# The entry of a two-layer hybrid decoder: another way to sum the squares of x, multiplications of zeros at the start, and the second chunk of a projection ahead of the decay's small matmuls

## The chip, the core and the metric

One core of one Trainium2 chip. The metric is the device time of one execution in microseconds (us); the lower, the better. The kernel before has three timed runs, and one more execution that was profiled.

## What is computed

The input x has 256 tokens of 2048 channels. Two layers follow each other, each a mixer and a squared-ReLU MLP, with an RMSNorm before and after each. Only the first steps of layer 0 matter here:

```
y    = x * rsqrt(mean(x^2 over channels) + eps) * w       # rmsnorm
proj = y @ w_in                                           # 2048 x 8208
q,k,v,z | beta,a | ... = split(proj)                      # gated DeltaNet and retention
g    = -exp(a_log) * softplus(a + dt_bias)                # decay, 8 heads
G    = cumsum(g) in chunks;  decay = exp(G_t - G_s)       # used by the delta rule
```

The factor rsqrt(...) is one number per token, so it can be put on after the product `x*w @ w_in`, when the result is taken out of PSUM. The kernel does that: the product starts on x itself, and the factor (`rstd`, one column per block of 128 tokens) is needed only when the first results leave PSUM.

## The kernel before

All matmuls of the projections are float32 split in two: ScalarE rounds a weight tile `raw` to `whi` (line 125), VectorE subtracts to get the rest `wlo` (line 126), and TensorE makes three products of each tile, `xh*whi`, `xl*whi` and `xh*wlo` (lines 132, 133, 134). x is split in the same way into `xh` (ScalarE, line 192) and `xl` (VectorE, line 193).

A chunk of the projection is some 384 to 512 columns wide. It runs over 16 tiles of 128 channels, in four weight groups of four tiles, and over two blocks of 128 tokens: 96 matmuls. A weight group is one DMA from HBM on SyncE's queue, or several for the first groups (`PARTS`: four for the first, two for the second, one for each of the others). There are three `raw` buffers, so a group's DMA waits until VectorE has made the `wlo` of the group three before it.

The entry of layer 0 (`layer0_mixer`) loads x transposed (`xT`, eight DMAs of two channel tiles each into tiles `xs` with the tag kq), splits it, and makes the first chunk, 400 columns: 16 for beta and the decay and 384 of the gate z. GpSimd squares each `xs` tile (lines 512 and 515) and adds the squares to `sq` (line 516, tag Bn). When the last is added, four matmuls with a column of ones (line 527) sum `sq` over channels, and `rstd` follows (lines 530 and 185). The first chunk then leaves PSUM, and a chain of small steps on VectorE and ScalarE makes the decay `g`. One small matmul (line 569) sums it up, and 16 more (line 585, in four banks) spread it for the 256 exponentials' tiles.

The second chunk of the entry (384 more columns of z) stands behind these small matmuls in the program's text. A list scheduler of the framework fixes the order of each engine's queue when the kernel is built: of what it takes to be ready it puts the earliest in the text first. In the trace the second chunk's matmuls start before the decay is ready, and the small matmuls stand among them. Then come the chunks for k, q and v of the delta rule.

Of the kernel before, what the change touches and what calls it, by code (L numbers as in the profile page):

```python
# [12 lines left out]
AF = mybir.ActivationFunctionType  # L13
ALU = mybir.AluOpType
# [3 lines left out]
P = 128  # L18
D = 2048
SEQ = 256  # L20
HID = 4 * D
SGW = 2 * D
EPS = 1e-6
# [6 lines left out]
PARTS = [4, 2, 1, 1]  # L30
WAIT = [26, 30]
AHEAD = 200
SEVEN, KEPT = (0, 2), 1
ORDER = (None, 0, None, 1, None, 2, None, 3)
FIRST = (None, None, 1, None, 0, None, 3, 2)
# [58 lines left out]
def program(tc, nc, A, S):  # L94
    wp = tc.alloc_tile_pool(name="wp", bufs=1)
    cp = tc.alloc_tile_pool(name="cp", bufs=1)
# [5 lines left out]
    mxp = tc.alloc_tile_pool(name="mxp", bufs=2, space=PSUM)  # L102
    V, G, ACT, PE, DMA = nc.vector, nc.gpsimd, nc.scalar, nc.tensor, nc.sync
# [3 lines left out]
    def T(pool, shape, tag, dt=F32, bufs=None):  # L107
        uid[0] += 1
        kw = {} if bufs is None else {"bufs": bufs}
        return pool.tile(shape, dt, tag=tag, name=f"{tag}_{uid[0]}", **kw)  # L110

    def bank(pool, n, tag):
        return T(pool, [P, 512], tag)[:, :n]

    def weights(s, blocks, parts=1):
        src, width = s.take(blocks)
        raw = T(wp, [P, 2048], "raw", bufs=RAW_BUFS)[:, :width]
        hi = T(wp, [P, 2048], "whi", F32R, bufs=HI_BUFS)[:, :width]
        lo = T(wp, [P, 2048], "wlo", F32R, bufs=LO_BUFS)[:, :width]
        with tc.high_priority(offset=ahead[0]):  # L120
            n = width // parts
            for c in range(0, width, n):
                r, a, d = raw[:, c : c + n], hi[:, c : c + n], lo[:, c : c + n]
                DMA.dma_start(r, src[:, c : c + n])
                ACT.activation(a, r, AF.Copy)  # L125
                V.tensor_tensor(d, r, a.bitcast(F32), ALU.subtract)  # L126
        return hi, lo

    def prod_tok(ps, x, b, w, j, n, first, last):
        xh, xl = x[0][:, b * P : (b + 1) * P], x[1][:, b * P : (b + 1) * P]  # L130
        wh, wl = w[0][:, j * n : (j + 1) * n], w[1][:, j * n : (j + 1) * n]
        PE.matmul(ps, xh, wh, start=first, stop=False)  # L132
        PE.matmul(ps, xl, wh, start=False, stop=False)  # L133
        PE.matmul(ps, xh, wl, start=False, stop=last)  # L134
# [7 lines left out]
    def tick():  # L142
        clock[0] += 1
        while queue and queue[0][0] <= clock[0]:
            gen = heapq.heappop(queue)[2]
            delay = next(gen, None)
            if delay is not None:
                spawn(delay, gen)
# [6 lines left out]
    def chunk_tok(s, X, rows, spans, n, ps=None, first=True, last=True):  # L155
        if ps is None:
            ps = [bank(acc, n, "acc") for _ in range(2)]
        for u in range(0, len(rows), 4):
            w = weights(s, [(r, spans) for r in rows[u : u + 4]])
            for j in range(4):  # L160
                k = u + j
                for b in range(2):
                    prod_tok(ps[b], X[k], b, w, j, n, first and k == 0, last and k == len(rows) - 1)
                tick()
        return ps
# [10 lines left out]
    one = T(cp, [P, 1], "one")  # L176
# [3 lines left out]
    def small(n, tag, bufs=4):  # L180
        return T(cp, [P, n], tag, bufs=bufs)

    def rsqrt(out, x):
        n = x.shape[1]
        G.tensor_tensor(out, x, m05[:, :n], ALU.pow)

    def split(hi, lo, src, col=None):
        if col is None:
            ACT.activation(hi, src, AF.Copy)  # L189
            V.tensor_tensor(lo, src, hi.bitcast(F32), ALU.subtract)  # L190
        else:
            ACT.activation(hi, src, AF.Copy, scale=col)
            V.scalar_tensor_tensor(lo, src, col, hi.bitcast(F32), ALU.mult, ALU.subtract)
# [4 lines left out]
    def kts(groups):  # L198
        return [(e[0][:, j, :], e[1][:, j, :]) for e in groups for j in range(4)]
# [105 lines left out]
    ALLK = [k * P for k in range(NKT)]  # L305
# [181 lines left out]
    def layer0_mixer():  # L487
        rstd = [T(cp, [P, 1], f"rh{b}", bufs=2) for b in range(2)]
        s = S["la_in"]
        with tc.tile_pool(name="l0", bufs=1, reuse_waits="tile") as lp:  # L490
            xg = new_x()
            X = kts(xg)
            spans0 = [(4096, 16), (3072, 384)]
            ps = [bank(acc, 400, "acc") for _ in range(2)]
            xs = [T(lp, [P, 2, SEQ], "kq", bufs=8) for _ in range(8)]
            sq = T(lp, [P, 2, SEQ], "Bn", bufs=1)

            def load_x(i):
                DMA.dma_start(xs[i], A["xT"][:, i * 512 : (i + 1) * 512].rearrange("p (a t) -> p a t", a=2))
# [3 lines left out]
            for g in range(4):  # L503
                w = weights(s, [(r, spans0) for r in ALLK[g * 4 : g * 4 + 4]], parts=PARTS[g])
                for i in range(2 * g, 2 * g + 2):
                    if i < 7:
                        load_x(i + 1)
                    for a in range(2):
                        k = 2 * i + a
                        split(X[k][0], X[k][1], xs[i][:, a, :], nwc[:, k : k + 1])  # L510
                    if i == 0:
                        G.tensor_tensor(sq, xs[i], xs[i], ALU.mult)
                    else:
                        t = T(lp, [P, 2, SEQ], "PT", bufs=2)
                        G.tensor_tensor(t, xs[i], xs[i], ALU.mult)
                        G.tensor_tensor(sq, sq, t, ALU.add)
                if g == 3:
                    DMA.dma_start(ident, A["cst"][:, C_IDENT : C_IDENT + P])
                    lc = T(lp, [P, C_END - P], "lc")
                    DMA.dma_start(lc, A["cst"][:, P:C_END])  # L520
                for j in range(4):
                    for b in range(2):
                        prod_tok(ps[b], X[g * 4 + j], b, w, j, 400, g + j == 0, g * 4 + j == NKT - 1)
            pss = bank(mxp, 2, "mx")
            for b in range(2):
                for a in range(2):
                    PE.matmul(pss[:, b : b + 1], sq[:, a, b * P : (b + 1) * P], one, start=a == 0, stop=a == 1)
            for b in range(2):
                var = small(1, "var")
                V.tensor_scalar(var, pss[:, b : b + 1], 1.0 / D, EPS, ALU.mult, ALU.add)  # L530
                rsqrt(rstd[b], var)
            tri = lc[:, C_TRI - P : C_TRI]
            neg = lc[:, C_NEG - P : C_NEG]
            mk = [lc[:, C_M1 - P : C_M1], lc[:, C_M2 - P : C_M2]]
# [3 lines left out]
            zt = [[None] * 4 for _ in range(2)]  # L538
# [41 lines left out]
            for b in range(2):  # L580
                for hg in range(2):
                    ps4 = bank(mxp, 512, "mx")
                    for q in range(4):
                        c = (hg * 4 + q) * 2 + b
                        PE.matmul(ps4[:, q * P : (q + 1) * P], g2[:, c : c + 1].to_broadcast([P, P]), tri,
                                  start=True, stop=True)
# [11 lines left out]
                    for q in range(4):  # L598
                        c = (hg * 4 + q) * 2 + b
                        ACT.activation(e4[:, q, :], e4[:, q, :], AF.Exp, bias=ngc[:, c : c + 1])  # L600
            last_exp = ACT.activation(etail, etail, AF.Exp)

            ps = chunk_tok(s, X, ALLK, [(3072 + 384, 384)], 384)
            for b in range(2):
                ACT.activation(zt[b][0][:, 384:512], ps[b][:, 0:128], AF.Copy, scale=rstd[b])
                ACT.activation(zt[b][1][:, 0:256], ps[b][:, 128:384], AF.Copy, scale=rstd[b])
            with tc.issue_after(last_exp.ins):
                for b in range(2):
                    ACT.activation(zt[b][0], zt[b][0], AF.Silu)
# [255 lines left out]
            RQ, RK, RV, RG = 4112, 5136, 6160, 7184  # L865
            ahead[0] = AHEAD
            GT = [
# [20 lines left out]
            ps = chunk_tok(s, X, ALLK, [(3072 + 768, 256)], 256)  # L888
# [102 lines left out]
            for c in range(4):  # L991
                ps = chunk_tok(so, Og, ALLK[:12], [(c * 512, 512)], 512)
# [14 lines left out]
    def layer1_mixer(X, rh):  # L1007
        si, so = S["sg_in"], S["sg_out"]
        with tc.tile_pool(name="sg", bufs=1, reuse_waits="tile") as gp:
# [75 lines left out]
            return down_last(so, gts[7], rows(7), w1, w0, lambda b: rows_in(["e0", "e1"]), None)  # L1085

    X, rh, rv = layer0_mixer()
    X, rh, rv = ffn(S["up0"], S["dn0"], X, rv, 1, 5)
    X, rh, rv = layer1_mixer(X, rh)
# [58 lines left out]
```

## Time and profile before

| what | us |
|---|---|
| median of three runs | 2547.78 (2545.24 to 2547.9) |
| the profiled execution | 2548.88 |
| its span, first to last instruction | 2547.1 |
| TensorE busy in it | 2506.0 (98%) |
| VectorE, ScalarE, GpSimd busy | 1968.8, 1201.2, 285.8 |

The span is what the rows below are taken from. The profiled execution lasted 1.8 us longer than its span. Matmuls are pipelined, and their ends are modelled; so the distance from one start to the next tells more of TensorE's pace than the duration does.

### The profile page before, as it was taken

How to read it: one execution, taken by the hardware profiler on the slowest of the kernel's cores; microseconds unless marked ns; L12 is line 12 of the kernel's file. 1: busy time of each engine (PE TensorE's matmuls, PEld its weight loads, DVE VectorE, ACT ScalarE, POOL GpSimd, SP SyncE). 2: the span in 40 equal slices, each digit the busy share in tenths (PEclk: the TensorE clock that was granted, in tenths of full speed). 3: DMA queues.
4: the chain of work that ended last, by engine and by line, in shares of the span. 5: the costliest groups of instructions: out<-in, count | busy, mean ns of one | idle time of the engine just before them, and what ended most of it. 6: DMA issues, size and time to landing. Idle time of an engine off the chain costs nothing.

```text
span 2547.1 us, 36465 instructions
## 1 busy us (share of the span) xinstructions
PE 2506.0 (98%) x15138; PEld 2211.3 (87%) x15138; DVE 1968.8 (77%) x2256; ACT 1201.2 (47%) x1174; POOL 285.8 (11%) x222
## 2 busy tenths in 40 slices
PE   8999999999999999999999999999999999999998
PEld 7778888878999999999878877777789999999997
DVE  7586855579888888888854596876898888888887
ACT  6555444454454454545544333333544544445453
POOL 3000201140000000000310110110400000000001
PEclk9999999999999999999999999999999999999999
DMA  6444544544555455555555455555445554555553
GB/s 245 181 151 147 187 162 175 204 155 174 195 195 199 183 204 192 190 192 205 204 204 194 170 203 202 190 202 199 149 165 199 189 206 185 198 192 189 191 201 139
DMA packets 81255, 478.04 MB, mean 188 GB/s; under 512 B 13633, under 2 KB 15809, under 8 KB 26817
## 3 DMA queue, kind: packets, MB, share of 16 engines
q1 hardware_dynamic: 81088, 475.70, 51.1%
q8 instruction: 119, 1.95, 0.3%
q14 instruction: 48, 0.39, 0.0%
HBM read 473.04 MB, written 2.62 MB: 187 GB/s over the span
## 4 chain that ended last, share of the span: by engine, by line
PE 45%; DVE 4%; POOL 1%; issue 1%; ACT 0%; DVEq 0%; POOLq 0%; ACTq 0%
PE acc L133 9%; PE acc L134 9%; PE acc L132 9%; PE tp L318 4%; PE tp L319 4%; PE tp L320 4%; PE acc L362 1%; PE acc L364 1%; PE acc L363 1%; DVE wlo L126 1%; PE mx L363 1%; PE mx L362 1%; PE mx L364 1%; DVE h L275 1%; DVE bc L218 1%
## 5 line engine op out<-in xcount | busy, mean ns | idle before, releaser
L126 DVE TENSOR_TENSOR wlo<-raw,whi 128x2048 fp32r<-128x2048 f32 (+3 forms) x380 | 860.3, 2267 | 269.1 <-ACT whi L125 267.1
L125 ACT ACTIVATE whi<-raw 128x2048 fp32r<-128x2048 f32 (+3 forms) x380 | 714.1, 1880 | 566.3 <-PE acc L133 319.2
L318 PE MATMUL tp<-xh,whi 128*128 128x256 f32 x1920 | 539.5, 281 | 0.0
L319 PE MATMUL tp<-xl,whi 128*128 128x256 f32 x1920 | 539.2, 281 | 0.0
L320 PE MATMUL tp<-xh,wlo 128*128 128x256 f32 x1920 | 538.9, 281 | 0.0
L132 PE MATMUL acc<-whi,xh 128*128 128x512 f32 (+3 forms) x1120 | 446.3, 398 | 5.8 <-ACT whi L125 5.8
L134 PE MATMUL acc<-wlo,xh 128*128 128x512 f32 (+3 forms) x1120 | 440.0, 393 | 5.1 <-DVE wlo L126 5.1
L133 PE MATMUL acc<-whi,xl 128*128 128x512 f32 (+3 forms) x1120 | 438.9, 392 | 0.0
L318 PEld LDWEIGHTS tp<-xh,whi 128*128 128x128 f32 x1920 | 361.5, 188 | 2.7
L319 PEld LDWEIGHTS tp<-xl,whi 128*128 128x128 f32 x1920 | 361.6, 188 | 2.5
L320 PEld LDWEIGHTS tp<-xh,wlo 128*128 128x128 f32 x1920 | 361.7, 188 | 0.0
L134 PEld LDWEIGHTS acc<-wlo,xh 128*128 128x128 f32 x1120 | 212.1, 189 | 53.2 <-DVE wlo L126 7.0
L132 PEld LDWEIGHTS acc<-whi,xh 128*128 128x128 f32 x1120 | 212.4, 190 | 51.8 <-ACT whi L125 6.3
L133 PEld LDWEIGHTS acc<-whi,xl 128*128 128x128 f32 x1120 | 212.3, 190 | 44.7 <-issue 1.0
L387 POOL TENSOR_TENSOR rl<-rl 128x512 f32<-128x512 f32 x64 | 83.0, 1313 | 1261.0 <-ACT rl L386 1136.3
L189 ACT ACTIVATE whi<-qsum 128x2048 fp32r<-128x2048 f32 x60 | 115.3, 1922 | 179.9 <-DVE qsum L343 178.9
L190 DVE TENSOR_TENSOR wlo<-qsum,whi 128x2048 fp32r<-128x2048 f32 x60 | 138.7, 2312 | 79.0 <-ACT whi L189 77.0
L416 DVE TENSOR_TENSOR y<-acc,y 128x512 f32<-128x512 f32 x112 | 76.9, 687 | 86.1 <-PE acc L364 86.1
L189 ACT ACTIVATE whi<-raw 128x1536 fp32r<-128x1536 f32 x60 | 89.6, 1493 | 108.2 <-DMA raw<-dn 79.0
L133 PE MATMUL acc<-whi,e1l 128*128 128x512 f32 x288 | 114.0, 396 | 0.0
L134 PE MATMUL acc<-wlo,e1h 128*128 128x512 f32 x288 | 113.8, 395 | 0.0
L132 PE MATMUL acc<-whi,e1h 128*128 128x512 f32 x288 | 113.7, 395 | 0.0
(350 smaller groups left out, 4212.8 us busy)
## 6 DMA issues: line engine op xcount, KB each, us to landing
raw<-up SPq DMA_DIRECT2D x128, 1024.0 KB, 4.8
raw<-dn SPq DMA_DIRECT2D x128, 1024.0 KB, 4.8
raw<-sg_in SPq DMA_DIRECT2D x64, 1024.0 KB, 4.8
raw<-la_in SPq DMA_DIRECT2D x56, 1024.0 KB, 4.8
raw<-sg_out SPq DMA_DIRECT2D x32, 1024.0 KB, 4.8
raw<-la_out SPq DMA_DIRECT2D x16, 1024.0 KB, 4.8
raw<-la_in SPq DMA_DIRECT2D x4, 768.0 KB, 4.4
kq<-xT SPq DMA_DIRECT2D x8, 256.0 KB, 6.1
```

What stands on the lines that cost most here:

```text
L125: ACT.activation(a, r, AF.Copy)
L126: V.tensor_tensor(d, r, a.bitcast(F32), ALU.subtract)
L132: PE.matmul(ps, xh, wh, start=first, stop=False)
L133: PE.matmul(ps, xl, wh, start=False, stop=False)
L134: PE.matmul(ps, xh, wl, start=False, stop=last)
L189: ACT.activation(hi, src, AF.Copy)
L190: V.tensor_tensor(lo, src, hi.bitcast(F32), ALU.subtract)
L318: PE.matmul(out, wh[:, col], xh, start=k == 0 and m % 2 == 0, stop=False, skip_group_check=True)
L319: PE.matmul(out, wh[:, col], xl, start=False, stop=False, skip_group_check=True)
L320: PE.matmul(out, wl[:, col], xh, start=False, stop=k == NKT - 1, skip_group_check=True)
L387: G.tensor_tensor(r, r, r, ALU.mult)
L416: V.tensor_tensor(Y[key], ps, Y[key], ALU.add)
```

## The change

Four things. GpSimd no longer squares x. Behind the first chunk's loop x is loaded a second time, token-major, in four DMAs of 128 tokens by 1024 channels, and ScalarE squares each with a sum over its row (`accum_out`). The tiles have the tag PT, of which there are two buffers. `rstd` is made from the two sums of each token block, so that the four matmuls of line 527 are gone. Ten matmuls of a 128x128 tile of zeros are put at the very start (`WARM`), into a PSUM bank that nothing reads. The second chunk is moved in the text from behind the decay to ahead of it; its results are taken out where they were before.

```diff
+WARM = 10
...
             xs = [T(lp, [P, 2, SEQ], "kq", bufs=8) for _ in range(8)]
-            sq = T(lp, [P, 2, SEQ], "Bn", bufs=1)
+            heat = T(cp, [P, P], "heat")
+            G.memset(heat, 0.0)
+            cold = bank(mxp, P, "mx")
+            for _ in range(WARM):
+                PE.matmul(cold, heat, heat, start=True, stop=True)
...
                         split(X[k][0], X[k][1], xs[i][:, a, :], nwc[:, k : k + 1])
-                    if i == 0:
-                        G.tensor_tensor(sq, xs[i], xs[i], ALU.mult)
-                    else:
-                        t = T(lp, [P, 2, SEQ], "PT", bufs=2)
-                        G.tensor_tensor(t, xs[i], xs[i], ALU.mult)
-                        G.tensor_tensor(sq, sq, t, ALU.add)
...
-            pss = bank(mxp, 2, "mx")
             for b in range(2):
-                for a in range(2):
-                    PE.matmul(pss[:, b : b + 1], sq[:, a, b * P : (b + 1) * P], one, start=a == 0, stop=a == 1)
-            for b in range(2):
-                var = small(1, "var")
-                V.tensor_scalar(var, pss[:, b : b + 1], 1.0 / D, EPS, ALU.mult, ALU.add)
+                ssx = small(2, "ssx")
+                for c in range(2):
+                    xt = T(lp, [P, 1024], "PT", bufs=2)
+                    DMA.dma_start(xt, A["x"][b * P : (b + 1) * P, c * 1024 : (c + 1) * 1024])
+                    ACT.activation(xt, xt, AF.Square, accum_out=ssx[:, c : c + 1])
+                base, var = small(1, "base"), small(1, "var")
+                V.tensor_scalar(base, ssx[:, 0:1], 1.0 / D, EPS, ALU.mult, ALU.add)
+                V.tensor_scalar(var, ssx[:, 1:2], 1.0 / D, base, ALU.mult, ALU.add)
                 rsqrt(rstd[b], var)
+            psz = chunk_tok(s, X, ALLK, [(3072 + 384, 384)], 384)
...
             last_exp = ACT.activation(etail, etail, AF.Exp)
 
-            ps = chunk_tok(s, X, ALLK, [(3072 + 384, 384)], 384)
             for b in range(2):
-                ACT.activation(zt[b][0][:, 384:512], ps[b][:, 0:128], AF.Copy, scale=rstd[b])
-                ACT.activation(zt[b][1][:, 0:256], ps[b][:, 128:384], AF.Copy, scale=rstd[b])
+                ACT.activation(zt[b][0][:, 384:512], psz[b][:, 0:128], AF.Copy, scale=rstd[b])
+                ACT.activation(zt[b][1][:, 0:256], psz[b][:, 128:384], AF.Copy, scale=rstd[b])
```

## Rows read from the trace of the kernel before

**Rows 1.** The page's first part: busy time, share of the span, instructions.
```profile
PE 2506.0 (98%) x15138; PEld 2211.3 (87%) x15138; DVE 1968.8 (77%) x2256; ACT 1201.2 (47%) x1174; POOL 285.8 (11%) x222
```

**Rows 2.** Engine busy time by stretch: PE, PEld, DVE, ACT, POOL; TensorE's clock; DMA share, GB/s.
```profile
10.00:15.00 5.00, 3.66 (x13) 3.33 (x12) 5.00 (x5) 3.45 (x6) 4.84 (x4) 1.00 0.99 388
25.00:30.00 5.00, 3.67 (x12) 3.64 (x13) 5.00 (x6) 1.48 (x1) 3.51 (x2) 0.66 0.44 157
40.00:45.00 5.00, 5.00 (x35) 4.73 (x34) 4.26 (x12) 4.95 (x6) 0.00 (x0) 1.00 0.66 249
```

**Rows 3.** Who waited for whom in the first 38 us: total, times, longest.
```profile
ACT whi L125 <- DMA raw<-la_in: 9.4, 5, 3.6
PE acc L134 <- DVE wlo L126: 5.1, 4, 2.6
```

**Rows 4.** VectorE in order of time: start, duration of all merged, instruction.
```profile
4.51 0.98 DVE L193 SCALAR_TENSOR_TENSOR xl<-kq,par,xh 128x256 fp32r<-128x256 f32 x2 [3.55 <-ACT xh L192]
5.42 0.56 DVE L126 TENSOR_TENSOR wlo<-raw,whi 128x400 fp32r<-128x400 f32 x1
10.26 2.92 DVE L193 SCALAR_TENSOR_TENSOR xl<-kq,par,xh 128x256 fp32r<-128x256 f32 x2
13.10 3.40 DVE L126 TENSOR_TENSOR wlo<-raw,whi 128x400 fp32r<-128x400 f32 x2
29.59 1.81 DVE L126 TENSOR_TENSOR wlo<-raw,whi 128x1600 fp32r<-128x1600 f32 x1
31.32 0.87 DVE L193 SCALAR_TENSOR_TENSOR xl<-kq,par,xh 128x256 fp32r<-128x256 f32 x2
```

**Rows 5.** GpSimd's groups in the first 38 us: count, busy us and mean ns.
```profile
L516 POOL TENSOR_TENSOR Bn<-Bn,PT 128x512 f32<-128x512 f32 x7 | 10.4, 1484 | 0.5
L515 POOL TENSOR_TENSOR PT<-kq 128x512 f32<-128x512 f32 x7 | 10.4, 1482 | 2.8 <-DMA kq<-xT 2.8
```

**Rows 6.** TensorE in order of time, the matmuls alone.
```profile
5.36 0.70 PE L132 MATMUL acc<-whi,xh 128*128 128x400 f32 x1 [5.36 <-ACT whi L125]
14.85 0.34 PE L132 MATMUL acc<-whi,xh 128*128 128x400 f32 x1
...
15.04 0.35 PE L133 MATMUL acc<-whi,xl 128*128 128x400 f32 x1
...
17.06 0.54 PE L132 MATMUL acc<-whi,xh 128*128 128x400 f32 x1
...
17.39 0.54 PE L133 MATMUL acc<-whi,xl 128*128 128x400 f32 x1
...
36.01 0.95 PE L527 MATMUL mx<-one,Bn 128*128 128x1 f32 x8
36.82 0.42 PE L132 MATMUL acc<-whi,xh 128*128 128x384 f32 x1
...
43.19 0.40 PE L569 MATMUL mx<-g,lc 128*128 128x16 f32 x2
43.44 2.03 PE L585 MATMUL mx<-lc,g 128*128 128x128 f32 x16
```

**Rows 7.** SyncE's queue in order of time: start, time to issue, DMA.
```profile
7.93 1.19 SPq L499 DMA_DIRECT2D kq<-xT  x2
14.54 0.33 SPq L124 DMA_DIRECT2D raw<-la_in  x1
```

**Rows 8.** ScalarE in order of time.
```profile
9.41 0.53 ACT L125 ACTIVATE whi<-raw 128x400 fp32r<-128x400 f32 x1
15.12 1.54 ACT L125 ACTIVATE whi<-raw 128x1600 fp32r<-128x1600 f32 x1 [0.97 <-DMA raw<-la_in]
20.09 1.54 ACT L125 ACTIVATE whi<-raw 128x1600 fp32r<-128x1600 f32 x1 [1.83 <-DMA raw<-la_in]
```

**Rows 9.** ScalarE's groups of the whole span: a pass over 1024 columns, and the accumulator's reading.
```profile
L189 ACT ACTIVATE f0h<-tr 128x1024 fp32r<-128x1024 f32 x16 | 16.8, 1047 | 6.8 <-DVE tr L401 6.8
L227 ACT ACTIVATION_READ_ACCUMULATOR junk<-y 128x1 f32 x32 | 6.0, 188 | 0.0
```

## Prediction

> **What bounds the kernel now.** The page's busy shares come first: TensorE has 2506.0 of 2547.1 us [rows 1]. All that is not TensorE's is 41 us, so an edit can win only where TensorE waits or runs at a low clock. The table by stretches shows one such place in the entry. From 10 to 15 us and from 25 to 30 us TensorE is busy 3.66 and 3.67 of 5 us, and the clock granted falls to 0.66 in the second; from 40 us on it is busy all the time at 1.00 [rows 2]. In both early stretches VectorE is busy 5.00 of 5 us, and GpSimd 4.84 and 3.51 [rows 2]. The waits of the entry say the same: TensorE waits for VectorE's `wlo` [rows 3].
>
> VectorE's order of time shows why it is full. Two `xl` of 128x256 take 0.98 us at 4.51 and 0.87 us at 31.32, but 2.92 us at 10.26: 1.46 us each in place of some 0.46. A `wlo` of 400 columns takes 0.56 us at 5.42; at 13.10 one of 400 and one of 800 columns (the row names the first) take 3.40 us [rows 4], where 0.56 + 1.0 would be expected from the widths. Between 10 and 28 us GpSimd runs its squares and sums, 15 operations of 1.0 to 1.5 us [rows 5]. When they are over, 1600 columns take 1.81 us [rows 4], which is the pace of the first 400. So the slow stretch is the one in which both engines work.
>
> The first chunk ends where line 527 starts, at 36.01 us, and the second begins at 36.82 [rows 6]. What the change is worth is how much earlier the second chunk begins, if TensorE then stays full, as it does now.
>
> **The squares leave GpSimd.** I take VectorE's prices from the undisturbed rows: 0.46 us for an `xl`, 1.81 us for a group's `wlo`. What is late next? The fourth weight group's DMA waits for VectorE to have read the first group's last part. That part is rounded at 9.94 (9.41 + 0.53) [rows 8], the pair of subtractions starts at 13.10 [rows 4], and the DMA is issued at 14.54 [rows 7]. Undisturbed, the subtraction ends near 10.6 and the DMA is issued near 11, while the queue is still working. The third group has landed at 15.12 [rows 8]. Ahead of the fourth in the queue are then two more `xT` loads issued at 7.93 [rows 7]. These and the fourth group are 0.52 + 0.82 = 1.34 MB, at the 388 GB/s of 10 to 15 us [rows 2] 3.5 us: it lands at 18.6 in place of 20.09 [rows 8]. ScalarE's 1.54 us give `whi` at 20.1.
>
> The greater gain is behind that. Now `wlo` of the fourth group is made from 29.59 to 31.40 [rows 4], 9.5 us after `whi` was begun at 20.09 [rows 8], since other subtractions stand before it. After the change the third `wlo` is ready at 15.12 + 1.54 + 1.81 = 18.5 us, four `xl` take to 20.4, the fourth `wlo` to 22.2, the last two `xl` to 23.1. TensorE then sets the end: of the 48 matmuls of the third and fourth groups two, which need only `whi`, are done at 18.5; the other 46 at a distance of 0.19 us, that of the fast level (14.85 to 15.04 [rows 6]), are 8.7 us: 27.2. From below, TensorE is held by the third `whi` alone (15.12 + 1.54 = 16.7) and ends at 16.7 + 48 x 0.19 = 25.8. From above, all 46 have the distance of the slow level, 0.33 (17.06 to 17.39 [rows 6]), and end at 33.7. I take the fast level, because TensorE then has its operands without a wait but at one or two places.
>
> **Line 527 goes.** From 36.01 to 36.82 is 0.81 us, a matmul's distance included, so 0.6 are won: the second chunk starts at 27.2 in place of 36.82. Together **-9.6 us**.
>
> **The second load of x.** Four DMAs of 0.52 MB, 2.1 MB, at 388 GB/s 5.4 us of the queue. Where SyncE issues them is not in this trace. By the text they come after the constants and before the second chunk's weights, and the second pair waits for the squares of the first, as there are two buffers. I take the first pair ahead of the second chunk's first group, the second pair behind it. Behind the fourth group (18.6) are then `xT` 0.26, constants 0.46, the pair 1.05 and the group 0.79 MB: 2.56 MB, 6.6 us, 25.2. Rounding (at most the 1.54 us of 1600 columns) gives `whi` at 26.7, `wlo` at 28.5. TensorE has four products that need only `whi`, to 27.9, and waits **0.6 us**. The lower bound is nothing (the pair later), the upper 5.4 us (all four ahead).
>
> **The squares on ScalarE.** Four passes of 1.05 us and the accumulator's 0.19 [rows 9], 5.0 us. ScalarE waits 9.4 us for weights in the entry [rows 3]; between 21 and 32 us it has besides only two `whi`. Nothing, while that cover stands; else up to one pass, 1.2 us, for each `whi` that stands behind a square. VectorE's four small steps and GpSimd's power are the work of lines 530 and 185, one step more for each block: nothing, hidden by the second chunk.
>
> **Zeros.** GpSimd's fill is at most some 0.5 us. A 128x128 matmul of line 585 is two records of 0.127 us (2.03 / 16 [rows 6]), so ten are 2.5 us at the fast level and 5.1 at half of it. From some 1.3 us on they end between 3.8 and 6.4 us; the first real matmul now starts at 5.36 [rows 6]. They can delay it by 1.0. TensorE needs 48 x 0.19 = 9.1 us for the first two groups and has until 16.7, so the delay is hidden, and a faster clock there wins nothing either. Without that cover the delay is +1.0; the fast level at the third group is in my 27.2 already.
>
> The row that speaks against warming up is in the trace: fast matmuls at 14.85 are slow again at 17.06, after waits for `wlo` [rows 6, 3]. The Trainium skill, "TensorE: Matmul & The Clock Gate", section "HAM oscillation — how this bites in real kernels", has it as a rule: a kernel whose matmuls wait for a DMA at each step falls back to half rate in each. By it the zeros are lost at the first wait, and the entry would run slow to its end. That is the second rival below.
>
> **The second chunk first.** The same 96 and 17 small matmuls in another order. The small ones cost TensorE 0.25 us for line 569 (43.19 to 43.44) and some 2 us for each two of the four banks of line 585 [rows 6], before and after. If the decay is ready when they come, nothing; it is not a gain, as they stand without a wait now.
>
> **Sum.** -9.6 + 0.6 = -9.0 us against the profiled execution's 2548.9 (2547.1 of span and 1.8 around it): 2539.9. The median of the runs lies 1.1 us lower, at 2547.8, so I predict 2538.8 us. A difference under 0.2% (5.1 us) can't be told from no change here.
>
> **Rivals.**
> 1. The transfers become the bound. For it: the DMA share is 0.99 from 10 to 15 us [rows 2], and 2.1 MB are added there. Against: it is 0.44 from 25 to 30 [rows 2]. If all four loads stand ahead of the second chunk's weights, or the first pair ahead of the fourth group, the 5.4 us are lost: gain 4 us, 2543.8. Chance 0.19.
> 2. The clock stays low through the first chunk: it ends at 33.7 and the second begins there, with its weights in place: gain 3.1, 2544.7. For it the slow distance at 17.06, against it that from 18.5 on TensorE hardly waits. Chance 0.08.
> 3. The change does not free VectorE, as something else slows it (the transfers, say, at 388 GB/s). Then only line 527's 0.6 us are won: 2547.2. Against it: from 25 to 30 us the transfers are down to 157 GB/s, and VectorE is still full [rows 2]. Chance 0.07.
> 4. Slower: TensorE stands at line 569 in its fixed order. The decay needs both blocks' sums, and so the last of the four loads, which waits in SyncE's queue. Now 7 us lie between the end of the first chunk and line 569 (36.01 to 43.19 [rows 6]). The second chunk would end at 27.8 + 96 x 0.18 = 45.1, so the last square must be done by 37.9. By my queue it is at 31: 25.2, another group and the second pair (1.84 MB, 4.7 us), a square. Each us later than 37.9 costs one. At a slip of 6.9 + 9.0 = 16 us the gain is gone; slower by 0.2% it is from 21 us on, 2552.9 and more. For it: the fourth group's issue at 14.54 shows that SyncE holds all that stands behind a waiting DMA [rows 7]. Against: the last load would have to stand behind four more weight groups or so. Chance 0.05.
>
> The forecast, a gain of 7 to 12 us, has 0.61; half of the first rival's cases are over 5.1 us. So faster 0.70, same 0.25, slower 0.05. The fastest case is the 25.8 us from below with no wait, a gain of 11, and less than the 2.7 us that lie between the runs: 2535. The range reaches up to the second rival: 2535 to 2545.
>
> **What would show it.** Right: VectorE's `xl` at 0.5 us throughout; the fourth `wlo` at 20 to 22 us; no line 527; the second chunk's first matmul at 26 to 28 us; line 569 near 45 us without a wait ahead of it; the rest of the span as before, 9 us earlier. Wrong: `xl` still over 1 us; ScalarE or TensorE idle for `raw` between 25 and 35 us with the DMA share near 1; matmuls at 0.33 us after 20 us; a wait before line 569; or new waits in the chunks of k, q and v, whose order the builder draws anew.

## The result, and the profile after

The changed kernel is slower: 2557.09 us (median of six runs, 2555.51 to 2560.4) against 2546.52 us of the kernel before beside it (six runs, 2545.03 to 2549.46). The ratio is 1.0042, interval 1.0029 to 1.0054: 10.6 us more, where 9.0 less were forecast. Its profiled execution has a span of 2558.7 us.

The first part of the profile's page of the changed kernel answers to [rows 1]:

```profile
span 2558.7 us, 36491 instructions
...
PE 2523.6 (99%) x15150; PEld 2229.8 (87%) x15150; DVE 1939.4 (76%) x2258; ACT 1208.0 (47%) x1184; POOL 264.7 (10%) x208
```

TensorE is busy 17.6 us longer, with twelve instructions more. The multiplications of zeros are 4.6 us of that. The other 13 us are not work that the change added: the same matmuls took longer.

Where were they lost? First the entry. The table by stretches of the changed kernel answers to [rows 2] and has the same columns:

```profile
10.00:15.00 5.00, 5.00 (x29) 5.00 (x28) 4.12 (x8) 3.56 (x7) 0.00 (x0) 1.00 1.01 397
15.00:20.00 5.00, 3.99 (x21) 3.31 (x20) 3.52 (x6) 4.84 (x7) 0.00 (x0) 1.00 1.04 406
20.00:25.00 5.00, 5.00 (x29) 5.00 (x28) 2.79 (x5) 2.85 (x6) 0.55 (x1) 1.00 0.91 336
25.00:30.00 5.00, 2.66 (x14) 2.00 (x12) 1.73 (x2) 2.99 (x4) 0.00 (x0) 0.97 0.86 297
30.00:35.00 5.00, 4.68 (x15) 4.68 (x16) 1.20 (x6) 2.77 (x5) 0.56 (x1) 0.50 0.85 321
```

VectorE is no longer full, and the granted clock is 1.00 until 25 us. TensorE is held for about 1 us between 15 and 20 us, where the forecast had its wait for the third `wlo`, and again from 25 us on. VectorE in order of time (answers to [rows 4]), then TensorE (to [rows 6]), then ScalarE (to [rows 8]), all of the changed kernel, where lines are numbered one higher:

```profile
11.97 0.88 DVE L194 SCALAR_TENSOR_TENSOR xl<-kq,par,xh 128x256 fp32r<-128x256 f32 x2
...
19.80 1.82 DVE L127 TENSOR_TENSOR wlo<-raw,whi 128x1600 fp32r<-128x1600 f32 x1
...
28.50 1.76 DVE L127 TENSOR_TENSOR wlo<-raw,whi 128x1536 fp32r<-128x1536 f32 x1 [2.02 <-ACT whi L126]
```

```profile
1.06 4.64 PE L501 MATMUL mx<-heat 128*128 128x128 f32 x20 [1.06 <-POOL heat L498]
...
5.81 0.34 PE L134 MATMUL acc<-whi,xl 128*128 128x400 f32 x1
5.99 0.35 PE L133 MATMUL acc<-whi,xh 128*128 128x400 f32 x1
...
26.34 0.35 PE L135 MATMUL acc<-wlo,xh 128*128 128x400 f32 x1
28.52 0.45 PE L133 MATMUL acc<-whi,xh 128*128 128x384 f32 x1 [1.83 <-ACT whi L126]
...
30.32 1.01 PE L135 MATMUL acc<-wlo,xh 128*128 128x384 f32 x2 [0.82 <-DVE base L530]
31.12 0.52 PE L133 MATMUL acc<-whi,xh 128*128 128x384 f32 x1
31.45 0.52 PE L134 MATMUL acc<-whi,xl 128*128 128x384 f32 x1
...
36.54 0.34 PE L135 MATMUL acc<-wlo,xh 128*128 128x384 f32 x1
36.72 0.34 PE L133 MATMUL acc<-whi,xh 128*128 128x384 f32 x1
```

```profile
26.52 0.58 ACT L547 ACTIVATE y<-acc,rh 128x384 f32<-128x384 f32 x1 [2.73 <-DVE ab L546]
27.00 1.47 ACT L126 ACTIVATE whi<-raw 128x1536 fp32r<-128x1536 f32 x1
```

Who waited for whom in the first 38 us (to [rows 3]), and SyncE's queue (to [rows 7]):

```profile
PE acc L133 <- ACT whi L126: 3.1, 3, 1.8
...
ACT whi L126 <- DMA raw<-la_in: 1.7, 4, 0.9
```

```profile
10.58 0.33 SPq L125 DMA_DIRECT2D raw<-la_in  x1
...
12.93 2.29 SPq L527 DMA_DIRECT2D PT<-x  x2
15.64 0.33 SPq L125 DMA_DIRECT2D raw<-la_in  x1
22.55 1.59 SPq L527 DMA_DIRECT2D PT<-x  x2
```

The fourth weight group is issued at 10.58 (forecast 11, before 14.54), the first pair of x loads stands ahead of the second chunk's first group and the second pair behind it, as I took it. ScalarE's waits for transfers fall from 9.4 to 1.7 us. Two `xl` take 0.88 us, the fourth `wlo` is ready at 21.6, and the first chunk is through at 26.5 us, all nearly as forecast. The second chunk does not follow at once: its first weights are rounded only at 27.00, because ScalarE takes its instructions in order, and line 547 (the first chunk's way out of PSUM) stands ahead of them and waits 2.73 us for the first chunk's end. TensorE loses 2.0 us there and 1.0 at 30.32. The second wait is put down to `base`, a step of VectorE; the `wlo` just before it, made from 28.50 to 30.26 out of that late rounding, is what these matmuls read. After that the matmuls are 0.32 us apart until 36.5 (18 of them, 0.145 too much each, 2.6 us).

So the entry wins less than 9 us; but it wins. The 96th matmul of 512 columns has the same matmuls ahead of it in both kernels, the zeros and line 527 apart. It starts at 80.03 us before and at 75.29 in the changed kernel:

```profile
80.03 0.40 PE L134 MATMUL acc<-wlo,xh 128*128 128x512 f32 x1
```

```profile
75.29 0.40 PE L135 MATMUL acc<-wlo,xh 128*128 128x512 f32 x1
```

The loss comes later. The view of one source line has the first and the last start of an instruction. This is the first product of the up-pass in MLP 0, in the kernel before and in the changed one:

```profile
L318 PE MATMUL tp<-xh,whi x960: 277/281/285, 576.8 to 1234.1; 128*128 128x256 f32 x192
```

```profile
L319 PE MATMUL tp<-xh,whi x960: 278/281/286, 573.1 to 1237.9; 128*128 128x256 f32 x192
```

The changed kernel comes to MLP 0 with 3.7 us won, and has 3.8 us lost when the last of these starts: the same stretch takes 664.8 us in place of 657.3. No code of it was changed. From one start to the next, the mean over the 2880 matmuls of that up-pass is 118.26 ns before and 119.99 ns after. I use this distance below as the pace.

### The profile page after: what moved, and what is told of

Same layout as the page of the kernel before. It is cut to its first block, busy times and chain, and to the rows that moved or that the text cites. A ratio compares the mean times of both kernels' runs of the same rounds, so it can differ in the third digit from the quotient of the medians.

```text
span 2558.7 us, 36491 instructions
## 1 busy us (share of the span) xinstructions
PE 2523.6 (99%) x15150; PEld 2229.8 (87%) x15150; DVE 1939.4 (76%) x2258; ACT 1208.0 (47%) x1184; POOL 264.7 (10%) x208
## 4 chain that ended last, share of the span: by engine, by line
PE 46%; DVE 4%; issue 1%; POOL 1%; ACT 0%; DVEq 0%; POOLq 0%; ACTq 0%
PE acc L133 9%; PE acc L135 9%; PE acc L134 9%; PE tp L319 4%; PE tp L320 4%; PE tp L321 4%; PE acc L363 1%; PE acc L365 1%; PE acc L364 1%; DVE wlo L127 1%; PE mx L364 1%; PE mx L365 1%; PE mx L363 1%; DVE bc L219 1%; DVE h L276 1%
```

## Experiments: why TensorE is slower everywhere

Three theories. **A**: the place of the operands. The zeros (512 bytes per partition) and the partial sums (four buffers of 32 bytes) are new tiles in a pool ahead of the split x, so that by the built program's allocation the split x begins at byte 97504 of each partition in place of 96864, and all that is allocated behind it moves by the same 640 bytes; the weight buffers stay. **B**: the added work, or the order that the builder draws anew. **C**: the chip at hand.

**The place alone.** The kernel before, and one tile that nobody uses:

```diff
             xs = [T(lp, [P, 2, SEQ], "kq", bufs=8) for _ in range(8)]
+            G.memset(T(cp, [P, 160], "pad"), 0.0)
```

> The kernel before, with one unused tile of 640 bytes per partition ahead of the tiles of x, the hidden state and the MLP, as the zeros and the two sums of the changed kernel take (512 and 128); GpSimd fills it once. Nothing else is changed. If the place of the tiles in SBUF slows TensorE (theory A), the matmuls of the MLP stand 1.4% further apart from about 590 us on and the kernel takes some 16 us more than before, 2562. If it is the new order of the instructions or the added work (theory B), or a chip that was slower in the changed kernel's profile (theory C), it takes what the kernel before takes, 2546 to 2548.

Measured: 2563.07 us against 2546.88, ratio 1.0063 (1.0048 to 1.0078). The same view of that kernel:

```profile
L318 PE MATMUL tp<-xh,whi x960: 278/281/285, 577.3 to 1242.1; 128*128 128x256 f32 x192
```

664.8 us, the changed kernel's number, and the pace is 119.99 ns. 640 unused bytes cost 16.2 us. In its trace TensorE, VectorE and ScalarE have the instructions of the kernel before in the same order, and GpSimd has one more, the pad's filling. A holds; B and C can't explain it.

**The change without the shift.** The zeros lie in a buffer that is used later anyway, and the sums in one that is there already:

```diff
-            heat = T(cp, [P, P], "heat")
+            heat = T(lp, [P, SEQ], "cv", bufs=2)[:, :P]
...
-                ssx = small(2, "ssx")
+                ssx = small(4, "ss")
```

> The changed kernel in its own order, instruction for instruction, but the zeros lie in a buffer of the layer's pool that is free then and the sums in small buffers that exist already, so that the weights' tiles and the tiles of x lie where they lay before. Theory A: the pace of the matmuls is that of before, 118.3 and 233.3 ns apart, the 4.8 us won by 80 us stay to the end, and it takes 2541 to 2543. Theory B or C: it takes what the changed kernel takes, 2556 to 2558.

Measured: 2541.6 us, ratio 0.998 (0.997 to 0.9989), 5.3 us faster than the kernel before and 15.5 faster than the changed one. In its trace every engine has the changed kernel's instructions in the changed kernel's order. Pace 118.26 ns:

```profile
L319 PE MATMUL tp<-xh,whi x960: 277/281/285, 569.5 to 1225.9; 128*128 128x256 f32 x192
```

**Which of the two tiles.** Each edit of the last diff by itself: first the sums alone (512 bytes of shift are left), then the zeros alone (128 are left).

> The changed kernel with one edit: the partial sums of the squares come from the pool's existing four-wide tag, so that 128 bytes per partition less lie ahead of the split x; the zeros keep their own 512 bytes. Theory A (the place of TensorE's operands, where 128 bytes count and 512 do not): 2540 to 2543.5 us, as with both tiles moved, and the 256-column matmuls of MLP 0 at 118.2 ns. Rival (the distance from the weights, or the sum of the bytes, sets the pace): about four fifths of the loss stays, 2551 to 2556 us, matmuls between 119 and 120 ns.

> The changed kernel with the other edit alone: the zeros lie in a buffer that comes later in memory, the partial sums keep their own tag, so everything behind moves by 128 bytes and not by 640. Theory A: as slow as the changed kernel, 2555 to 2561 us, 256-column matmuls at 119.9 to 120.1 ns. Rival (sum of the bytes): a fifth of the loss, 2543 to 2546 us, 118.5 ns.

Measured: 2540.82 us (0.9976, 0.9966 to 0.9985) with 512 bytes, 2558.47 (1.0044, 1.0028 to 1.006) with 128. The two in the same view:

```profile
L319 PE MATMUL tp<-xh,whi x960: 276/281/285, 572.2 to 1229.7; 128*128 128x256 f32 x192
```

```profile
L319 PE MATMUL tp<-xh,whi x960: 277/282/287, 572.0 to 1235.2; 128*128 128x256 f32 x192
```

657.5 and 663.2 us, paces 118.25 and 119.95. So it is not the number of bytes. One edit in one line (the tag and the width of a tile of two numbers) decides the sign of the change.

**What law.** The kernel before with other pads (`[P, 128]`, `[P, 64]`, `[P, 104]` in place of `[P, 160]`), one run each:

> The kernel before with an unused tile of 512 bytes per partition, the size of the zeros alone. Theory A with the place counted in steps of 1024 bytes or more: slower than before, by an amount that is not the same as with 640. If only the place within 512 bytes matters, the pace is exactly that of before, 118.3 ns in the MLP, and the time 2546 to 2548.

> The kernel before, and 256 unused bytes per partition ahead of the split x, so that it begins at 352 bytes past a multiple of 512 and not at 96. If the place counts within 256 bytes: 2546 to 2549 us and 118.2 to 118.3 ns for a 256-column matmul of MLP 0. If it counts within 512: another pace than 118.25, on either side, 2540 to 2565 us.

> The kernel before, and 416 unused bytes per partition, so that the split x and all tiles behind it begin at a multiple of 512. If a row that begins on such a boundary is read best: under 118.25 ns for a 256-column matmul, 2530 to 2546 us. If only the distance from other tiles counts: any pace from 118 to 120.5 ns, 2545 to 2566 us. If nothing but the shift of 128 bytes matters: 118.25 ns, 2547 us.

Where the split x begins, as the rest of its byte address by 512, and the pace:

| kernel | rest by 512 | rest by 256 | ns from start to start | time, us |
|---|---|---|---|---|
| before | 96 | 96 | 118.26 | 2546.5 |
| 512 bytes more | 96 | 96 | 118.25 | 2546.81 |
| 256 bytes more | 352 | 96 | 118.25 | 2546.85 |
| 416 bytes more | 0 | 0 | 118.65 | 2547.53 |
| 128 bytes more (zeros moved) | 224 | 224 | 119.95 | 2558.47 |
| 640 bytes more | 224 | 224 | 119.99 | 2563.07 |

Within 256 bytes the place counts, 256 or 512 bytes more change nothing. A round address is not the best one for these matmuls, but it is for others: from 570 to 1240 us, distances over 300 ns left out, the 512-column matmuls start 233.2 ns apart before, 234.1 with 640 bytes more and 232.3 with 416. So one place can cost one kind of matmul and win at another, and the time shows the sum. In the up-pass the tile that moved is the one that streams through TensorE and the weights that are loaded stayed in place; in the 512-column matmuls it is the other way round. The Trainium skill, "SBUF — State Buffer", section "Operand start alignment", asks of an operand only that it start at a multiple of its element's size, and gives no speed for it; all these places fulfil that, and the measured paces differ by 1.5%. Which tile has to lie well, the split x or one of those that move with it, is open, as they all moved together here; so is whether its own address counts or its distance from another tile that is read or written at the same time.

## Experiments: why the entry won 5 us and not 9

All of these keep the places of before, so their times are read against 2541.6 us; the kernel before took 2546.1 to 2546.9 beside each.

**GpSimd's work put back.** The 15 operations on x, into buffers that nobody reads:

```diff
+            sq = T(lp, [P, 2, SEQ], "Bn", bufs=1)
...
+                    if i == 0:
+                        G.tensor_tensor(sq, xs[i], xs[i], ALU.mult)
+                    else:
+                        t = T(lp, [P, 512], f"Um{i % 2}", bufs=1).rearrange("p (a t) -> p a t", a=2)
+                        G.tensor_tensor(t, xs[i], xs[i], ALU.mult)
+                        G.tensor_tensor(sq, sq, t, ALU.add)
```

> The changed kernel with the places of before, and GpSimd's 15 operations on x put back beside it; nobody uses their result. Theory (GpSimd's work slows VectorE, and leaving it out is what made the first chunk end early): the two-xl rows take 2 to 3 us again between 10 and 28 us, and the first chunk's last matmul starts at 32 to 36 us and not at 26. The second chunk then finds its weights ready, so the 4.4 us of its waits go against the loss: 2545 to 2549 us. Rival (ScalarE, the faster queue or the zeros made the first chunk early): xl stays near 0.9 us for two, the chunk ends near 26, 2541 to 2543 us.

Measured: 2550.83 us, ratio 1.002 (1.0011 to 1.003). VectorE, TensorE and ScalarE of that kernel, and one row of its table by stretches:

```profile
15.68 2.68 DVE L194 SCALAR_TENSOR_TENSOR xl<-kq,par,xh 128x256 fp32r<-128x256 f32 x2
...
30.57 0.87 DVE L194 SCALAR_TENSOR_TENSOR xl<-kq,par,xh 128x256 fp32r<-128x256 f32 x2
```

```profile
34.91 0.34 PE L135 MATMUL acc<-wlo,xh 128*128 128x400 f32 x1
37.09 0.44 PE L133 MATMUL acc<-whi,xh 128*128 128x384 f32 x1 [1.84 <-ACT whi L126]
```

```profile
35.09 0.58 ACT L555 ACTIVATE y<-acc,rh 128x384 f32<-128x384 f32 x1 [9.01 <-DVE ab L554]
35.56 1.47 ACT L126 ACTIVATE whi<-raw 128x1536 fp32r<-128x1536 f32 x1
```

```profile
35.00:40.00 5.00, 2.33 (x9) 1.76 (x8) 2.09 (x4) 4.03 (x6) 0.56 (x1) 0.89 0.05 15
```

The first chunk ends at 35.1 us, near the 36.0 of before, and the kernel is 9.2 us slower than without GpSimd's work: the first reason of the forecast stands. The Trainium skill, "SBUF — State Buffer", section "Who interferes with whom", has it: a VectorE instruction with two inputs from SBUF contends with a GpSimd instruction that reads SBUF. The trace agrees: 1.34 us for an `xl` beside GpSimd's work, 0.44 behind it.

I had expected 2545 to 2549 us, because the late first chunk would find the second chunk's weights ready and pay no waits; this was wrong, and it tells what the wait is. From 35 to 40 us the DMA share is 0.05, the weights lie there, and TensorE waits the same 1.84 us. ScalarE has idled 9.01 us at the head of its queue, at the first chunk's evacuation, with the rounding behind it.

**The evacuations behind the roundings.** On ScalarE the two evacuations are held until the second chunk's last rounding:

```diff
-                ACT.activation(zt[b][0][:, 0:384], ps[b][:, 16:400], AF.Copy, scale=rstd[b])
+                with tc.issue_after(whi_z.ins):
+                    ACT.activation(zt[b][0][:, 0:384], ps[b][:, 16:400], AF.Copy, scale=rstd[b])
```

> The changed kernel with the places of before, and the two evacuations of the first chunk on ScalarE held behind the last rounding of the second chunk's weights. Theory (ScalarE's order makes the second chunk's waits): TensorE waits no longer at the second chunk's first and second group for roundings that stand behind an evacuation; of the four waits there, 4.4 us in all, 2.5 to 4.4 go: 2537 to 2539.5 us. Rival (the weights' transfers are late, behind the loads of x): the waits stay and the releaser is the transfer; 2541 to 2543 us. A third case: TensorE gets to the decay's small matmuls before they are ready, and waits there for what it saved.

Measured: 2541.18 us, ratio 0.9977 (0.9967 to 0.9987), nothing won against 2541.6. ScalarE and TensorE:

```profile
25.59 1.49 ACT L127 ACTIVATE whi<-raw 128x1536 fp32r<-128x1536 f32 x1 [1.36 <-DMA raw<-la_in]
...
31.22 1.06 ACT L529 ACTIVATE PT<-PT 128x1024 f32<-128x1024 f32 x1 [3.10 <-DMA PT<-x]
...
33.55 0.22 ACT L557 ACTIVATE beta<-ab 128x16 f32<-128x16 f32 x1 [1.19 <-DVE ab L548]
33.68 2.84 ACT L127 ACTIVATE whi<-raw 128x1536 fp32r<-128x1536 f32 x2
```

```profile
35.20 0.45 PE L134 MATMUL acc<-whi,xh 128*128 128x384 f32 x1 [2.53 <-ACT whi L127]
```

The wait of 1.84 us at the first group is gone (the 0.82 for its `wlo` stayed), and one of 2.53 us has come at the second. Its rounding stands behind the step for beta, which waits for the second block's sum of squares, which waits for the last load of x; that pair was issued when the first squares had given their buffers back. The wait had moved along ScalarE's queue, to the next instruction in it that waits for something late.

**All of that chain out of the way.** The first pair of x loads keeps its two buffers, the second gets buffers that are free so early; the loads go behind the second chunk's second weight group, the squares behind its second rounding, evacuations, `ab` and beta behind the last one, and `dtb` and `alog` are loaded with the constants. The core of the edit:

```diff
+                if b == 1:
+                    xt = [T(lp, [P, 1024], "Bn", bufs=1)]
+                    xt += [T(lp, [P, 512], f"Um{i}", bufs=1) for i in range(2)]
...
+                    with tc.issue_after(raw_1.ins), tc.high_priority(offset=400):
+                        DMA.dma_start(t, A["x"][b * P : (b + 1) * P, o : o + n])
+                    with tc.issue_after(whi_1.ins), tc.high_priority(offset=400):
+                        ACT.activation(t, t, AF.Square, accum_out=ssx[:, c : c + 1])
```

> As the one that keeps the places, and the second chunk's weights are no longer held up: the four loads of x stand behind the second chunk's second weight group in SyncE's queue and have buffers of their own, ScalarE takes the first chunk out only behind the rounding of the second chunk's last group, and the two small loads for the decay are issued with the constants. If the missing part of the gain in the entry was the wait of the second chunk for its weights and the low clock after it, its first matmul follows the first chunk's last within 0.3 us, the distance stays at 0.18 us, and the end is 4 to 5 us ahead of the one that keeps the places: 2537 with theory A, 2552 without it. If the low clock at 30 us has another cause, nothing is won by it.

Measured: 2535.22 us (four runs, 2535.01 to 2535.74), ratio 0.9955 (0.9938 to 0.9971). It beats the kernel before by 11.7 us and the changed one by some 22. The passage from the first chunk to the second, and the stretches of that kernel:

```profile
26.21 0.35 PE L135 MATMUL acc<-wlo,xh 128*128 128x400 f32 x1
...
26.39 0.34 PE L133 MATMUL acc<-whi,xh 128*128 128x384 f32 x1
```

```profile
25.00:30.00 5.00, 5.00 (x30) 5.00 (x29) 2.44 (x4) 4.90 (x8) 0.55 (x1) 1.00 1.03 408
30.00:35.00 5.00, 5.00 (x30) 5.00 (x29) 2.10 (x4) 3.75 (x6) 0.56 (x1) 1.00 0.86 355
```

0.18 us lie between the chunks, one matmul's distance, and TensorE waits nowhere in the second. 6.4 us are won against 2541.6, where 4 to 5 were expected; the waits that it removes sum to 4.4 in that kernel's trace. In the traces the 96th matmul of 512 columns starts 5.3 us earlier (69.31 and 74.65). The rest could be the clock, which fell behind those waits in some of the traces (0.50 from 30 to 35 us in the changed kernel's) and not in others (1.00 with the places of before); that was not taken apart.

**Without the zeros**, and **with the second chunk in its old place**:

```diff
-            heat = T(lp, [P, SEQ], "cv", bufs=2)[:, :P]
-            G.memset(heat, 0.0)
-            cold = bank(mxp, P, "mx")
-            for _ in range(WARM):
-                PE.matmul(cold, heat, heat, start=True, stop=True)
```

> The changed kernel with the places of before and without the zeros and their matmuls. My theory of the entry: the first two weight groups' 48 matmuls then start near 5.4 us at the slow distance of 0.33, turn fast near 12.5 us, and are done near 18, when the third group's second part is ready anyway; from there nothing differs: 2541 to 2543 us, within 1 us of the kernel with the zeros. Rival (the zeros carry the clock through the entry): without them the slow distance returns after 17 us as in the kernel before, and 3 to 7 us are lost, 2545 to 2549 us.

> The changed kernel with the places of before, and the second chunk written behind the decay's small matmuls again. If the order of the two is worth nothing, as the prediction had it: 2540.5 to 2543 us. Rival (TensorE, which takes its instructions in order, now reaches the small matmuls before the second block's sum of squares is there, which the trace of the changed kernel shows at 31 to 32 us): a wait of 3 to 8 us ahead of them or ahead of the second chunk, 2544 to 2549 us.

Measured: 2541.98 us (0.998, 0.9971 to 0.999) and 2542.42 (0.9983, 0.9974 to 0.9992). Each is within 1 us of the kernel with both, and the intervals reach over 2 us to each side: the zeros and the new order are worth nothing that these runs can tell. The zeros do change the clock at the start. In the changed kernel the first matmuls stand 0.18 us apart from 5.81 us on; without the zeros they stand 0.33 apart, the distance of the slow level, until 13.2 us:

```profile
5.95 0.54 PE L134 MATMUL acc<-whi,xl 128*128 128x400 f32 x1
6.28 0.54 PE L135 MATMUL acc<-wlo,xh 128*128 128x400 f32 x1
```

The clock column of the tables says 1.00 from 5 to 10 us for both, so the distances are the better sign here. With the zeros TensorE only comes sooner to its wait for the third group's `wlo`: the first chunk's last matmul starts at 26.09 us with them and at 27.15 without.

With the second chunk in its old place, the builder puts the small matmuls between the second chunk's groups, the first of them at 37.7 us, when the sums are there.

## Why the prediction was wrong, point by point

- **The failed step** is the half sentence that the change is worth how much earlier the second chunk begins, "if TensorE then stays full, as it does now", and "the rest of the span as before" after it. TensorE stayed full; its pace did not stay. I looked at what the new tiles do to queues and engines, and not at where they push the others. Measured: 15.5 us between the changed kernel and the one with the places of before, and 16.2 us for the pad alone; my sum had nothing for it. No case that I had weighed went through the pace. The pace accounts for it: 5760 matmuls of 256 columns in the two up-passes by 1.73 ns are 10 us, some 5900 of 512 columns by 0.8 are 5.
- **VectorE freed, -9.6 us**: right. The first chunk ended at 26.5 (forecast 27.2), and giving GpSimd its work back costs 9.2 us. The reading of [rows 5] as operations of 1.0 to 1.5 us was loose, since that row has means and single ones lasted up to 2.6 us; nothing hung on it.
- **The second chunk's wait, +0.6 us**: mis-sized. The transfers were as I had them (the first group rounded from 25.59 where nothing stands ahead of it, forecast 25.2). But I counted for ScalarE only the squares as what a rounding could stand behind, and not the evacuation of the first chunk and the step for beta, which wait in the same queue. Measured: 2.0 + 1.0 us of waits and 2.6 of slow matmuls in the changed kernel; 4.4 of waits with the places of before. -9.6 + 4.4 = -5.2, against 5.3 measured there. That these agree to 0.1 us is luck: in that trace the second chunk could have started at 26.3, 0.9 earlier than forecast, and about as much was lost elsewhere.
- **Line 527, the zeros, the second chunk's place**: forecast 0.6, nothing and nothing. No run took line 527 alone; for the last two nothing was measured, within 2 us.
- **The rivals.** The first (transfers the bound) did not come: the DMA share is above 1.0 from 10 to 20 us, and the first chunk still ended before its forecast. The second (low clock in the first chunk) did not come there, but in the second chunk, at 0.50 from 30 to 35 us, after the two waits; matmuls at 0.32 us after 20 us were among the signs of being wrong. The third is refuted by the 9.2 us. The fourth, the one for slower, had the wrong place: line 569 (now 571) comes at 60.2 us, and TensorE does not wait there. That the kernel was slower was none of its doing.

## What to carry to other kernels

A new tile is a change to every tile allocated behind it: compare the distance of starts of a matmul far away from the edit before looking for the loss in the edit, and when they differ, try the old kernel with a pad and the new one without the shift. Put small new tiles in buffers that exist, or at the end. When work is moved to an engine with an in-order queue, list all that waits in that queue, and ask for each what it waits for and what stands behind it; an evacuation waits for the end of a chunk, and the next chunk's weights should not stand behind it.

## What was not expected of the hardware

TensorE's pace, with its operands ready and the clock granted in full, depends on where in SBUF they lie: 118.25 to 118.26 ns for a matmul of 256 columns at three places a multiple of 256 bytes apart, 118.65 at a fourth (one trace), and 119.95 to 119.99 at places 128 and 640 bytes on, in every trace that has them. On this kernel, in which TensorE is busy 98% of the time, 640 bytes were 0.6% of the whole.
